# Six column tiles ahead of each norm of the first block, the first transfers in another order, smaller GpSimd pieces, operands shifted by 32 bytes

## The chip, the cores and the metric

The kernel runs on one core of a Trainium2 chip. The core has five engines with queues of their own that run side by side and wait for each other by semaphores: TensorE (PE) multiplies and writes to PSUM, VectorE (DVE) and ScalarE (ACT) work element by element, GpSimd (POOL) helps with element-wise work in SBUF, and SyncE (SP) issues transfers. The metric is the time of one execution on the device in microseconds; of several, the median counts.

## The reference

One sequence of 256 positions with a width of 1024, in float32, goes through two blocks of two layers each. The change is in the first block. Cut to what matters, one of its layers computes

```
h = rms_norm(x, norm1_g)
proj = h @ w_in                     # 1024 x 10312: a (2048), index queries, keys, q, k, v, c, gates
a = causal_dwconv(a_val * sigmoid(a_gate), conf_conv_w) + conf_conv_b        # 31 taps
y_conf = silu(layer_norm(a)) @ w_conf_out
y_attn = dsa_attention(q, k, v, iq, ik, iw) @ w_attn_out                     # top 64 of the causal keys
y_sc = (c_b * causal_dwconv(c_c * c_x, sc_conv_w)) @ w_sc_out
x = x + (gated sum of y_conf, y_attn, y_sc) @ w_o
u = causal_dwconv(rms_norm(x, norm2_g) @ w_up, ffn_conv_w) + ffn_conv_b      # 3 taps
x = x + (silu(u_gate) * u_val) @ w_down                                      # 2816 inner columns
```

with `rms_norm(x, g) = x * rsqrt(mean(x * x) + 1e-6) * g` over the 1024 features of a position. The second block works on these 256 positions and 256 of a context; its very last feed-forward on the 256 positions alone.

## The kernel before

Activations lie transposed: 128 features on the partitions, 8 feature tiles (`KD`), and the positions (`S` = 256) along the free axis. A projection is done one column tile of 128 outputs at a time. `weights` (line 71) fetches one such tile of 128 x 1024 floats (512 KB) over SyncE's queue into one of four `wraw` buffers and splits it into two parts in the faster 32-bit format (float32r): ScalarE copies the rounded value to `whi`, and VectorE or GpSimd subtracts it from the original into `wlo`; each has three buffers. The operand is split in the same way, `oph` and `opl` (later `hh` and `hl`, and in the feed-forwards `dh` and `dl`). `mm` (line 95) then makes 24 matmuls for one column tile: for each of the 8 feature tiles `whi` with `oph` and `whi` with `opl`, and behind them 8 with `wlo` and `oph`. Of the three products that make up float32 accuracy the smallest, low by low, is left out. In the first block a matmul has 256 columns, in the second mostly 512.

`psum` (line 56) sets how many PSUM banks the column tiles and the attention use in a stage, and what share of the weight splits goes to GpSimd: every second one in the first half of a layer (`ps1a`), none in the second (`ps1b`, whose GpSimd splits the feed-forward's `dl` instead). `bank` (line 116) hands out the banks in rotation. Dependencies are tracked by bank in PSUM and by region in SBUF. Work off the main line (the 31 taps, rotary positions, index scores, top-k, softmax) stands in lists of small pieces with an estimated cost; each call of `weights` runs pieces up to a budget of 1600 ns (`run_side`). A scheduler then orders each engine's queue by readiness and priority; `high_priority` moves instructions ahead.

`opening` (line 230) begins each half layer. As the norm's factor `rb` depends on the position alone, a column tile can be multiplied before `rb` is known: `early` (line 204) splits x times the gain, without `rb`, and the tile is multiplied by `rb` in PSUM afterwards. The opening multiplies the first tile so, calls `rms` (line 186: two matmuls with a constant matrix add up the squares over the partitions, ScalarE takes an approximate inverse root, VectorE refines it), then forms the true operand `hn`, split into `hh` and `hl` for all later tiles, and multiplies the other tiles of the opening. It has four tiles in four banks ahead of w_in and three in five banks ahead of w_up. Each tile's multiply by `rb` is VectorE's.

At the start, the four transfers of x (two feature tiles each) alternate between SyncE's and ScalarE's queue, then come the vectors of layer 0 (`vec1[0]`, 490 columns with norm gains, taps and biases), `ident`, `const1` (864 KB of tables) and the weights. `early` and the squares of the norm (`sq_add`, line 159) alternate feature tile by feature tile. The context `z` and the vectors of the second block are loaded at the beginning of layer 1's second half in program order.

Of the kernel before, what the change touches and what calls it, by code (L numbers as in the profile page):

```python
# [21 lines left out]
P = 128  # L22
# [18 lines left out]
class Kern:  # L41
    def __init__(self, tc):
        self.tc = tc
        self.nc = tc.nc
        self.nsplit = 0
        self.pool_share = (0, 1)
        self.jobs = []
        self.job_rate = self.job_due = 0.0
        self.side_hi, self.side_lo = [], []
        self.budget = self.due = 0.0  # L50
        self.mmset, self.atset, self.ps = [], [], None
        self.imm = self.iat = 0
        self.acc, self.last = {}, {}
# [12 lines left out]
    def split(self, hi, lo, src, lo_eng=None):  # L66
        nc = self.nc
        nc.scalar.activation(hi, src, AF.Copy)  # L68
        (lo_eng or nc.vector).tensor_tensor(lo, src, hi.bitcast(F32), op=OP.subtract)  # L69

    def weights(self, src, kt=KD):

        nc = self.nc
# [6 lines left out]
        eng = nc.gpsimd if self.nsplit % of < share else nc.vector  # L80
# [14 lines left out]
    def mm(self, ps, w, xh, xl, kt=KD, k0=0, start=True, stop=True):  # L95

        nc = self.nc
        hi, lo = w
        for k in range(kt):
            nc.tensor.matmul(ps, hi[:, k], xh[:, k0 + k], start=start and k == 0, stop=False)  # L100
            nc.tensor.matmul(ps, hi[:, k], xl[:, k0 + k], start=False, stop=False)  # L101
        for k in range(kt):
            nc.tensor.matmul(ps, lo[:, k], xh[:, k0 + k], start=False, stop=stop and k == kt - 1)  # L103
# [100 lines left out]
def early(K, pool, x, vec, n, k):  # L204

    if k == 0:
        K.early = (pool.tile([P, KD, S], F32R, name="oph", tag="op2h"),
                   pool.tile([P, KD, S], F32R, name="opl", tag="op2l"))
# [6 lines left out]
def first_layer(K, l, A, xz, big, vec1, vec2, cpool, ctx2):  # L215
# [6 lines left out]
    with ExitStack() as ctx:  # L222
        def operand(pool=big, tag="op0"):
            return (pool.tile([P, KD, S], F32R, name="oph", tag=tag + "h"),
                    pool.tile([P, KD, S], F32R, name="opl", tag=tag + "l"))
# [4 lines left out]
        def opening(gname, srcs):  # L230


            banks = []
            for i, src in enumerate(srcs):
                ps = K.bank()[:, :S]
                K.mm(ps, K.weights(src), *K.early)
                if i == 0:
                    rb = K.rms()
                    hh, hl = operand()
                    for k in range(KD):  # L240
                        h = K.np.tile([P, S], F32, name="hn", bufs=3)
                        nc.vector.scalar_tensor_tensor(h, x[:, k], V(gname, k), rb, op0=OP.mult, op1=OP.mult)
                        K.split(hh[:, k], hl[:, k], h)
                nc.vector.tensor_tensor(ps, ps, rb, op=OP.mult)
                banks.append(ps)
            return banks, hh, hl

        with ExitStack() as actx:
            actx.enter_context(K.psum(f"ps1a_{l}", 4, 2, (1, 2)))
            K.budget = 1600.0  # L250
            first, hh, hl = opening("n1", [A["w_in"][l, W_A + i] for i in range(4)])
            if l == 0:
                constants1(K, cpool, A)
                for i in range(1, DEPTH):
                    nc.scalar.dma_start(vec1[i], A["vec1"][i])
# [324 lines left out]
        with ExitStack() as fctx:  # L580
            fctx.enter_context(K.psum(f"ps1b_{l}", 5, 1, (0, 1)))
            first, hh, hl = opening("n2", [A["w_up"][l, i] for i in range(3)])
            ff = fctx.enter_context(tc.tile_pool(name=f"ff1_{l}", bufs=1, reuse_waits="tile"))
            pad(ff, PAD_OP1)
            dh = ff.tile([P, NF, S], F32R, name="dh")
            dl = ff.tile([P, NF, S], F32R, name="dl")
            if l == DEPTH - 1:
# [4 lines left out]
                nc.scalar.dma_start(xz[:, :, S:], A["z"])  # L592
                for i in range(DEPTH):
                    nc.scalar.dma_start(vec2[i], A["vec2"][i])
            for j in range(NF):
# [19 lines left out]
                K.split(dh[:, j], dl[:, j], us[0], nc.gpsimd)  # L615
                if j == 2:
# [20 lines left out]
def constants(K, pool, A):  # L637
    nc = K.nc

    def load(name, shape):  # L640
        t = pool.tile(shape, F32, name=name)
        nc.scalar.dma_start(t, A[name])
        return t
    K.ident = load("ident", [P, P])
# [211 lines left out]
def feed_forward(K, A, x, l, f, T, first, jobs, vec, after, out=None):  # L856

    tc, nc = K.tc, K.nc
    with ExitStack() as ctx:
# [3 lines left out]
        dh = ff.tile([P, NF, T], F32R, name="dh")  # L863
        dl = ff.tile([P, NF, T], F32R, name="dl")
# [49 lines left out]
def pad(pool, size):  # L914

    if size:
        pool.tile([P, size // 4], F32, name="pad")

# [581 lines left out]
def two_blocks_kernel(ctx, tc, A, out):  # L1500
# [66 lines left out]
```

## Time and profile before

| | |
|---|---|
| median of 3 runs | 2945.33 us (2944.72 to 2951.25) |
| profiled execution | 2947.42 us |
| its span, first to last instruction | 2945.6 us |
| mean granted TensorE clock | 0.992 |
| TensorE matmul busy | 2853.4 us (97%), 18738 instructions |
| VectorE busy | 2126.6 us (72%), 3788 instructions |
| ScalarE busy | 1325.6 us (45%), 2189 instructions |
| GpSimd busy | 388.0 us (13%), 225 instructions |
| DMA | 447.64 MB, mean 152 GB/s |

The busy time of an engine is the union of its instructions. Matmuls are pipelined: their ends are modelled and one overlaps the next, so the pace is read from starts. The granted clock is TensorE's share of 2.4 GHz: 0.5 means 1.2 GHz. In the chain that ended last, TensorE has 73%, VectorE 15%, DMA 5% and ScalarE 4% of the span. In a timeline row the bracket says how long the engine was idle before and what ended that.

### The profile page before, as it was taken

Reading aid. Unit: us, or ns where it says so; the run is one execution under the profiler, and the core shown is the slowest. Engines: PE = TensorE matmul, PEld = TensorE weight load, DVE = VectorE, ACT = ScalarE, POOL = GpSimd, SP = SyncE. Lnnn points to the kernel's source line nnn. Section 1 sums busy time; section 2 is a strip of 40 time slices with the busy share of each in tenths; the row PEclk is TensorE's granted clock in tenths of the full one; section 3 lists DMA queues with packets and bytes.
Section 4 is the critical chain, followed back from the end, with each engine's and each line's share of the span. In section 5 each row is a group of like instructions: output and inputs, shape, how many; then the busy total and the mean of one; then the engine's idle time right before and its main releaser. Section 6 shows DMA issues by size and latency. Waiting matters only on the chain.

```text
span 2945.6 us, 47619 instructions
## 1 busy us (share of the span) xinstructions
PE 2853.4 (97%) x18738; PEld 2557.2 (87%) x18738; DVE 2126.6 (72%) x3788; ACT 1325.6 (45%) x2189; POOL 388.0 (13%) x225
## 2 busy tenths in 40 slices
PE   7989999999899999999999899999999999999999
PEld 7889999998899999888788579888888888877999
DVE  7999789789986897777657855777645554484664
ACT  4455666544546655422225454322233322365543
POOL 3333422033234210000000300000000000010000
PEclk9999999999999999999999999999999999999999
DMA  6445556654455576555542112455534444322455
GB/s 206 144 130 162 178 183 222 215 167 138 130 160 180 180 220 215 176 183 171 166 149 95 44 52 73 158 172 169 166 109 161 161 154 142 99 80 74 160 183 152
DMA packets 127935, 447.64 MB, mean 152 GB/s; under 512 B 14304, under 2 KB 19936, under 8 KB 127072
## 3 DMA queue, kind: packets, MB, share of 16 engines
q1 hardware_dynamic: 124672, 439.14, 47.1%
q10 hardware_dynamic: 3040, 5.48, 0.5%
q8 instruction: 147, 2.41, 0.3%
q14 instruction: 76, 0.62, 0.1%
HBM read 443.51 MB, written 1.05 MB: 151 GB/s over the span
## 4 chain that ended last, share of the span: by engine, by line
PE 73%; DVE 15%; DMA 5%; issue 4%; ACT 4%; POOL 0%; SPq 0%; DVEq 0%; ACTq 0%; POOLq 0%
PE mmb L100 21%; PE mmb L101 21%; PE mmb L103 21%; DVE wlo L69 4%; DMA mraw<-in_w_mod_dram 3%; DVE mjunk L770 2%; DMA wraw<-in_w_up_dram 2%; ACT whi L68 1%; PE outb L972 1%; PE atb L939 1%; DVE opl L69 1%; PE mmb L110 1%; PE mmb L111 1%; PE mmb L109 1%; DVE uu L610 1%
## 5 line engine op out<-in xcount | busy, mean ns | idle before, releaser
L68 ACT ACTIVATE whi<-wraw 128x1024 fp32r<-128x1024 f32 (+1 forms) x688 | 714.7, 1041 | 821.6 <-PE mmb L101 624.9
L69 DVE TENSOR_TENSOR wlo<-wraw,whi 128x1024 fp32r<-128x1024 f32 (+1 forms) x575 | 699.7, 1219 | 296.3 <-ACT whi L68 192.1
L100 PE MATMUL mmb<-oph,whi 128*128 128x256 f32 x2512 | 637.1, 290 | 20.8 <-ACT whi L68 12.5
L101 PE MATMUL mmb<-opl,whi 128*128 128x256 f32 x2512 | 630.4, 288 | 5.2 <-DVE opl L69 3.0
L100 PE MATMUL mmb<-hh,whi 128*128 128x512 f32 (+1 forms) x1776 | 613.2, 357 | 1.1 <-ACT whi L68 1.1
L101 PE MATMUL mmb<-hl,whi 128*128 128x512 f32 (+1 forms) x1776 | 610.3, 356 | 0.0
L100 PEld LDWEIGHTS mmb<-oph,whi 128*128 128x128 f32 x2512 | 487.6, 194 | 35.2 <-ACT whi L68 14.7
L101 PEld LDWEIGHTS mmb<-opl,whi 128*128 128x128 f32 x2512 | 488.0, 194 | 13.3 <-DVE opl L69 4.9
L770 DVE SCALAR_TENSOR_TENSOR mjunk<-mraw,cvec 128x1024 f32<-128x1024 f32 x256 | 315.2, 1231 | 223.5 <-DMA mraw<-in_w_mod_dram 217.6
L100 PEld LDWEIGHTS mmb<-hh,whi 128*128 128x128 f32 x1776 | 337.0, 190 | 54.5 <-issue 7.4
L103 PE MATMUL mmb<-hh,wlo 128*128 128x512 f32 (+1 forms) x1776 | 379.1, 355 | 3.2 <-DVE wlo L69 3.2
L101 PEld LDWEIGHTS mmb<-hl,whi 128*128 128x128 f32 x1776 | 336.9, 190 | 48.3 <-issue 2.9
L103 PE MATMUL mmb<-oph,wlo 128*128 128x256 f32 x2512 | 357.8, 285 | 4.0 <-DVE wlo L69 4.0
L69 POOL TENSOR_TENSOR wlo<-wraw,whi 128x1024 fp32r<-128x1024 f32 x113 | 286.1, 2533 | 487.7 <-ACT whi L68 415.9
L100 PE MATMUL mmb<-dh,whi 128*128 128x256 f32 (+1 forms) x1122 | 344.6, 329 | 3.3 <-ACT dh L68 3.3
L101 PE MATMUL mmb<-dl,whi 128*128 128x256 f32 (+1 forms) x1122 | 343.7, 328 | 1.3 <-POOL dl L69 1.3
L103 PEld LDWEIGHTS mmb<-hh,wlo 128*128 128x128 f32 x1776 | 297.9, 189 | 52.5 <-DVE wlo L69 5.3
L103 PEld LDWEIGHTS mmb<-oph,wlo 128*128 128x128 f32 x2512 | 326.7, 193 | 5.8 <-DVE wlo L69 5.2
L100 PEld LDWEIGHTS mmb<-dh,whi 128*128 128x128 f32 x1122 | 214.7, 191 | 22.3 <-ACT dh L68 3.7
L101 PEld LDWEIGHTS mmb<-dl,whi 128*128 128x128 f32 x1122 | 214.6, 191 | 19.9 <-POOL dl L69 1.7
L275 DVE SCALAR_TENSOR_TENSOR cvb<-u,vec,cvb 128x256 f32<-128x256 f32 x480 | 212.6, 481 | 3.5
L103 PE MATMUL mmb<-dh,wlo 128*128 128x256 f32 (+1 forms) x1122 | 210.5, 329 | 1.3 <-DVE wlo L69 1.2
(336 smaller groups left out, 2876.4 us busy)
## 6 DMA issues: line engine op xcount, KB each, us to landing
wraw<-in_w_ff_dram SPq DMA_DIRECT2D x208, 512.0 KB, 3.6
wraw<-in_w_in_dram SPq DMA_DIRECT2D x200, 512.0 KB, 3.6
mraw<-in_w_mod_dram SPq DMA_DIRECT2D x144, 512.0 KB, 4.2
wraw<-in_w_up_dram SPq DMA_DIRECT2D x88, 512.0 KB, 4.3
wraw<-in_w_y_dram SPq DMA_DIRECT2D x64, 512.0 KB, 3.5
wraw<-in_w_ff_dram SPq DMA_DIRECT2D x64, 448.0 KB, 3.4
wraw<-in_w_down_dram SPq DMA_DIRECT2D x32, 448.0 KB, 4.0
wraw<-in_w_down_dram SPq DMA_DIRECT2D x16, 512.0 KB, 4.3
```

The lines of the kernel that those rows point to most:

```text
L68: nc.scalar.activation(hi, src, AF.Copy)
L69: (lo_eng or nc.vector).tensor_tensor(lo, src, hi.bitcast(F32), op=OP.subtract)
L100: nc.tensor.matmul(ps, hi[:, k], xh[:, k0 + k], start=start and k == 0, stop=False)
L101: nc.tensor.matmul(ps, hi[:, k], xl[:, k0 + k], start=False, stop=False)
L103: nc.tensor.matmul(ps, lo[:, k], xh[:, k0 + k], start=False, stop=stop and k == kt - 1)
L109: nc.tensor.matmul(ps, hi[:, k], a, start=start, stop=False)
L110: nc.tensor.matmul(ps, hi[:, k], b, start=False, stop=False)
L111: nc.tensor.matmul(ps, lo[:, k], a, start=False, stop=stop)
L275: nc.vector.scalar_tensor_tensor(box[0], u[:, j, t:t + S], V("cw", 31 * j + t), box[0], op0=OP.mult, op1=OP.add)
L610: nc.vector.scalar_tensor_tensor(uu[:, d:], pe[:, :S - d], V("fw", 3 * t + 2 - d), uu[:, d:], op0=OP.mult, op1=OP.add)
L770: nc.vector.scalar_tensor_tensor(junk, raw, 1.0, K.cvec[:, e], op0=OP.mult, op1=OP.mult, accum_out=K.mods[l][:, e, 8 * m + k:8 * m + k + 1])
L939: nc.tensor.matmul(ps[:, :n], self.q[:, self.pair, tb * P:(tb + 1) * P], self.kpad[:, self.key(e), self.keys[0]:self.keys[1]], start=True, ...
```

## The change

- `opening` takes six column tiles for each norm, in four banks ahead of w_in and five ahead of w_up: tile i lies in bank i mod n, the later ones in the second half of a bank. Tiles 0 and 1 are multiplied for the first seven feature tiles each, then both for the eighth; behind them comes `rms`, the multiply of these two by `rb`, the true operand, and tiles 2 to 5.
- At the start the first eight columns of the vectors (the norm's gains) are fetched first, the first weight tile behind two of the four x transfers and in two halves with a split each, the other vectors behind x. `ident`, `const1` and layer 1's vectors are issued behind the last split of the operand. A Copy of one column right after the constants makes ScalarE load its table. The squares come behind all eight `early` steps.
- A weight split that GpSimd takes is subtracted in four pieces of two feature tiles.
- z and the second block's vectors are issued behind the first Silu of layer 1's feed-forward.
- The operands of 256 columns (first block, and `dh`, `dl` of the last feed-forward) start 32 bytes later, with 32 bytes more behind them.

```diff
+    def load(self, src, kt=KD, cut=KD):
         raw = self.wp.tile([P, KD, P], F32, name="wraw", bufs=4)
-        nc.sync.dma_start(raw[:, :kt], src)
+        cuts = [slice(k, min(k + cut, kt)) for k in range(0, kt, cut)]
+        for c in cuts:
+            nc.sync.dma_start(raw[:, c], src[:, c])
...
-            self.split(hi[:, :kt], lo[:, :kt], raw[:, :kt], eng)
+            if self.nsplit % of < share:
+                for c in cuts:
+                    nc.scalar.activation(hi[:, c], raw[:, c], AF.Copy)
+                for k in range(0, kt, 2):
+                    c = slice(k, min(k + 2, kt))
+                    nc.gpsimd.tensor_tensor(lo[:, c], raw[:, c], hi[:, c].bitcast(F32), op=OP.subtract)
+            else:
+                for c in cuts:
+                    self.split(hi[:, c], lo[:, c], raw[:, c])
...
-        def opening(gname, srcs):
-            banks = []
-            for i, src in enumerate(srcs):
-                ps = K.bank()[:, :S]
-                K.mm(ps, K.weights(src), *K.early)
-                if i == 0:
-                    rb = K.rms()
-                    hh, hl = operand()
-                    for k in range(KD):
...
+        def opening(gname, srcs, n):
+            banks = [K.bank() for _ in range(n)]
+            tiles = [banks[i % n][:, i // n * S:(i // n + 1) * S] for i in range(len(srcs))]
+            two = []
+            for i in range(2):
+                two.append(K.weights(srcs[i]))
+                K.mm(tiles[i], two[i], *K.early, ks=range(KD - 1))
+            for i in range(2):
+                K.mm(tiles[i], two[i], *K.early, ks=(KD - 1,))
+            rb = K.rms()
+            for ps in tiles[:2]:
                 nc.vector.tensor_tensor(ps, ps, rb, op=OP.mult)
+            hh, hl = operand()
+            for k in range(KD):
...
+                act = K.split(hh[:, k], hl[:, k], h)
+            for i, ps in enumerate(tiles[2:], 2):
+                K.mm(ps, K.weights(srcs[i]), *K.early)
+                nc.vector.tensor_tensor(ps, ps, rb, op=OP.mult)
+            K.imm = (K.imm + len(srcs) - n) % len(K.mmset)
+            return tiles, hh, hl, act
...
-            first, hh, hl = opening("n1", [A["w_in"][l, W_A + i] for i in range(4)])
+            first, hh, hl, act = opening("n1", [A["w_in"][l, W_A + i] for i in range(6)], 4)
             if l == 0:
-                constants1(K, cpool, A)
+                with tc.issue_after(act.ins):
+                    nc.scalar.dma_start(K.ident, A["ident"])
+                    constants1(K, cpool, A)
...
-            first, hh, hl = opening("n2", [A["w_up"][l, i] for i in range(3)])
+            first, hh, hl, _ = opening("n2", [A["w_up"][l, i] for i in range(6)], 5)
...
+                if j == 0 and l == DEPTH - 1:
+                    with tc.issue_after(act.ins):
+                        nc.scalar.dma_start(xz[:, :, S:], A["z"])
...
+    nc.scalar.activation(K.np.tile([P, 1], F32, name="nwarm", bufs=2), K.inv[:, 0:1], AF.Copy)
...
+def shifted(pool, shape, **kw):
+    n, w = shape
+    t = pool.tile([P, n * w + 16], F32R, **kw)
+    return t[:, 8:8 + n * w].rearrange("p (a b) -> p a b", b=w)
...
     with tc.high_priority(1000):
+        o, w = V1["n1"]
+        nc.sync.dma_start(vec1[0][:, :o + w], A["vec1"][0][:, :o + w])
         for k in range(0, KD, 2):
             (nc.scalar if k % 4 else nc.sync).dma_start(xz[:, k:k + 2, :S], A["x"][:, k:k + 2])
-        nc.sync.dma_start(vec1[0], A["vec1"][0])
+            if k == 2:
+                K.ahead.append(K.load(A["w_in"][0, W_A], cut=4))
+        nc.scalar.dma_start(vec1[0][:, o + w:], A["vec1"][0][:, o + w:])
     constants(K, keep, A)
     for k in range(KD):
         early(K, big, xz[:, :, :S], vec1[0], "n1", k)
+    for k in range(KD):
         K.sq_add(xz[:, k, :S], k)
```

## Rows read from the trace of the kernel before

**Rows 1.** The page, busy us, share of the span and instructions of each engine.

```profile
PE 2853.4 (97%) x18738; PEld 2557.2 (87%) x18738; DVE 2126.6 (72%) x3788; ACT 1325.6 (45%) x2189; POOL 388.0 (13%) x225
```

**Rows 2.** TensorE's groups by shape: count | busy us, mean ns | idle before.

```profile
L103 PE MATMUL mmb<-oph,wlo 128*128 128x256 f32 x2512 | 357.8, 285 | 4.0 <-DVE wlo L69 4.0
...
L103 PE MATMUL mmb<-dh,wlo 128*128 128x256 f32 x660 | 95.3, 286 | 0.0
```

**Rows 3.** Timeline of TensorE: start us, us, instruction, times in a row.

```profile
19.61 1.91 PE L103 MATMUL mmb<-oph,wlo 128*128 128x256 f32 x8
...
30.16 1.12 PE L103 MATMUL mmb<-oph,wlo 128*128 128x256 f32 x8
...
1203.05 1.98 PE L103 MATMUL mmb<-hh,wlo 128*128 128x512 f32 x8
1204.87 0.39 PE L100 MATMUL mmb<-hh,whi 128*128 128x512 f32 x1
```

**Rows 4.** Timeline of the start; last row: transfers, KB and us to landing.

```profile
1.75 0.46 SPq L1515 DMA_DIRECT2D vec<-in_vec_dram  x1
...
7.37 1.28 ACT L211 ACT_TABLE_LOAD   x1 [7.37 <-DMA vec<-in_vec_dram]
...
10.54 1.06 ACT L68 ACTIVATE whi<-wraw 128x1024 fp32r<-128x1024 f32 x1 [1.37 <-DMA wraw<-in_w_in_dram]
...
11.65 0.58 PE L100 MATMUL mmb<-oph,whi 128*128 128x256 f32 x1 [11.65 <-ACT whi L68]
...
vec<-in_vec_dram SPq DMA_DIRECT2D x1, 245.0 KB, 5.6
```

**Rows 5.** Timeline of TensorE where the norms' operands come late.

```profile
32.23 0.39 PE L100 MATMUL mmb<-oph,whi 128*128 128x256 f32 x1 [0.95 <-ACT th L291]
...
35.19 0.38 PE L100 MATMUL mmb<-oph,whi 128*128 128x256 f32 x1 [1.27 <-ACT oph L68]
...
38.03 0.41 PE L101 MATMUL mmb<-opl,whi 128*128 128x256 f32 x1
...
401.16 0.36 PE L100 MATMUL mmb<-oph,whi 128*128 128x256 f32 x1 [0.61 <-DVE xz L575]
...
603.21 0.39 PE L101 MATMUL mmb<-opl,whi 128*128 128x256 f32 x1 [1.62 <-DVE opl L212]
...
616.06 0.39 PE L100 MATMUL mmb<-oph,whi 128*128 128x256 f32 x1 [2.02 <-ACT th L291]
...
617.13 0.42 PE L101 MATMUL mmb<-opl,whi 128*128 128x256 f32 x1
...
985.56 0.36 PE L100 MATMUL mmb<-oph,whi 128*128 128x256 f32 x1 [0.87 <-DVE xz L575]
```

**Rows 6.** Windows: stretch, its us, then PE, PEld, DVE, ACT, POOL, PEclk, DMA.

```profile
37.00:205.00 168.00, 155.32 (x1179) 145.74 (x1180) 161.08 (x332) 70.89 (x114) 62.95 (x29) 0.97 0.48 148
618.00:785.00 167.00, 154.48 (x1179) 145.37 (x1179) 158.35 (x329) 71.53 (x111) 62.05 (x29) 0.97 0.48 149
```

**Rows 7.** VectorE 37 to 205: ns min/median/max, first and last start; then groups.

```profile
L317 DVE TENSOR_TENSOR iq<-iqr,const x2: 2719/2805/2891, 80.2 to 86.1; 128x512 f32<-128x512 f32 x2
L316 DVE TENSOR_TENSOR ish<-ish,const x2: 678/679/680, 93.4 to 98.3; 128x512 f32<-128x512 f32 x2
...
L69 DVE TENSOR_TENSOR wlo<-wraw,whi x56: 1196/1218/3417, 36.7 to 398.1; 128x1024 fp32r<-128x1024 f32 x56
...
L69 DVE TENSOR_TENSOR wlo<-wraw,whi 128x1024 fp32r<-128x1024 f32 x24 | 34.4, 1432 | 2.2 <-ACT whi L68 2.2
L418 DVE SCALAR_TENSOR_TENSOR ia<-rl,iw,ia 128x256 f32<-128x256 f32 x7 | 7.1, 1014 | 0.0
...
L418 DVE SCALAR_TENSOR_TENSOR ia<-rl,iw,const 128x256 f32<-128x256 f32 x1 | 0.5, 472 | 0.0
```

**Rows 8.** GpSimd's splits of weights (37 to 245) and of the feed-forward's operand.

```profile
L69 POOL TENSOR_TENSOR wlo<-wraw,whi x28: 2343/2407/3697, 41.5 to 241.7; 128x1024 fp32r<-128x1024 f32 x28
...
L69 POOL TENSOR_TENSOR dl<-uu,dh x44: 727/1205/1769, 420.3 to 1127.4; 128x256 fp32r<-128x256 f32 x44
```

More of the change, by code (lines that the diff above doesn't have):

```diff
@@ L52, in __init__ @@
         self.imm = self.iat = 0
-        self.acc, self.last = {}, {}
+        self.acc, self.last, self.ahead = {}, {}, []
     @contextmanager
@@ L67, in split @@
         nc = self.nc
-        nc.scalar.activation(hi, src, AF.Copy)
+        act = nc.scalar.activation(hi, src, AF.Copy)
         (lo_eng or nc.vector).tensor_tensor(lo, src, hi.bitcast(F32), op=OP.subtract)
+        return act
     def weights(self, src, kt=KD):
+        return self.ahead.pop() if self.ahead else self.load(src, kt)
+    def load(self, src, kt=KD, cut=KD):
         nc = self.nc
         raw = self.wp.tile([P, KD, P], F32, name="wraw", bufs=4)
-        nc.sync.dma_start(raw[:, :kt], src)
+        cuts = [slice(k, min(k + cut, kt)) for k in range(0, kt, cut)]
+        for c in cuts:
+            nc.sync.dma_start(raw[:, c], src[:, c])
         hi = self.wp.tile([P, KD, P], F32R, name="whi", bufs=3)
@@ L93, in run_side, with mm @@
         self.due = min(self.due, 0.0) if not (self.side_hi or self.side_lo) else self.due
-    def mm(self, ps, w, xh, xl, kt=KD, k0=0, start=True, stop=True):
+    def mm(self, ps, w, xh, xl, kt=KD, k0=0, start=True, stop=True, ks=None):
         nc = self.nc
         hi, lo = w
-        for k in range(kt):
+        ks = range(kt) if ks is None else ks
+        for k in ks:
             nc.tensor.matmul(ps, hi[:, k], xh[:, k0 + k], start=start and k == 0, stop=False)
             nc.tensor.matmul(ps, hi[:, k], xl[:, k0 + k], start=False, stop=False)
-        for k in range(kt):
+        for k in ks:
             nc.tensor.matmul(ps, lo[:, k], xh[:, k0 + k], start=False, stop=stop and k == kt - 1)
@@ L206, in early @@
     if k == 0:
-        K.early = (pool.tile([P, KD, S], F32R, name="oph", tag="op2h"),
-                   pool.tile([P, KD, S], F32R, name="opl", tag="op2l"))
+        K.early = (shifted(pool, [KD, S], name="oph", tag="op2h"),
+                   shifted(pool, [KD, S], name="opl", tag="op2l"))
     hh, hl = K.early
@@ L250, in first_layer @@
             K.budget = 1600.0
-            first, hh, hl = opening("n1", [A["w_in"][l, W_A + i] for i in range(4)])
+            first, hh, hl, act = opening("n1", [A["w_in"][l, W_A + i] for i in range(6)], 4)
             if l == 0:
-                constants1(K, cpool, A)
-                for i in range(1, DEPTH):
-                    nc.scalar.dma_start(vec1[i], A["vec1"][i])
+                with tc.issue_after(act.ins):
+                    nc.scalar.dma_start(K.ident, A["ident"])
+                    constants1(K, cpool, A)
+                    for i in range(1, DEPTH):
+                        nc.scalar.dma_start(vec1[i], A["vec1"][i])
             opp = actx.enter_context(tc.tile_pool(name=f"op1_{l}", bufs=1, reuse_waits="tile"))
@@ L615, in first_layer @@
                 K.split(dh[:, j], dl[:, j], us[0], nc.gpsimd)
+                if j == 0 and l == DEPTH - 1:
+                    with tc.issue_after(act.ins):
+                        nc.scalar.dma_start(xz[:, :, S:], A["z"])
+                        for i in range(DEPTH):
+                            nc.scalar.dma_start(vec2[i], A["vec2"][i])
                 if j == 2:
@@ L638, in constants @@
     nc = K.nc
[L640 to L644, printed above, removed]
+    K.ident = pool.tile([P, P], F32, name="ident")
     K.inv = pool.tile([P, P], F32, name="inv")
     nc.vector.memset(K.inv, 1.0 / 1024.0)
+    nc.scalar.activation(K.np.tile([P, 1], F32, name="nwarm", bufs=2), K.inv[:, 0:1], AF.Copy)
     K.magic = pool.tile([P, 64], I32, name="magic")
@@ L862, in feed_forward @@
         pad(ff, PAD_FF2)
-        dh = ff.tile([P, NF, T], F32R, name="dh")
-        dl = ff.tile([P, NF, T], F32R, name="dl")
+        dh = shifted(ff, [NF, T], name="dh") if T == S else ff.tile([P, NF, T], F32R, name="dh")
+        dl = shifted(ff, [NF, T], name="dl") if T == S else ff.tile([P, NF, T], F32R, name="dl")
         for j in range(NF):
```

19 lines of the change are left out of this document (6 added, 13 removed).

## The prediction

> **What bounds the kernel now.** I read the page's busy table, then TensorE's groups by shape, then its timeline where it stands idle, then the busy table of the two stages between the norm and the attention, and last VectorE and GpSimd there.
>
> TensorE is busy 97% of the span [rows 1], so its pace and its idle places count. The pace is flat: at full clock eight 256-column matmuls in a row last 1.12 us and a lone one 0.285 [rows 2, 3], so one starts every (1.12 − 0.285) / 7 = 0.119 us, 0.120 in round numbers; eight of 512 columns take 1204.87 − 1203.05 = 1.82, so 0.227 each; at half clock, where a lone one lasts 0.41 [rows 5], the 256-column ones start every (1.91 − 0.41) / 7 = 0.214 [rows 3].
>
> The idle places that the change touches are of three kinds. The start: nothing multiplies until 11.65 us, behind `vec` (245 KB, 5.6 us from issue to landing), a table load of 1.28 us that begins only when `vec` is there at 7.37, and the first weight tile, whose split begins at 10.54 [rows 4]. The places where the norm and its operand come late: 0.95 and 1.27 us in layer 0, 1.62 and 2.02 in layer 1, 0.61 and 0.87 ahead of w_up [rows 5]; behind the first two pairs the clock falls to 1.2 GHz (at 38.03 and 617.13 a matmul lasts 0.41 or 0.42). Third, the stages 37 to 205 and 618 to 785: TensorE works 155.3 of 168 us and 154.5 of 167 at a granted 0.97, VectorE 161.1 and 158.4 [rows 6]. There VectorE is the bound; TensorE's idle 12.7 and 12.5 us, and some 0.03 × 168 = 5 us of clock in each, are all there is to win.
>
> VectorE's time there is partly waiting. Operations with two SBUF inputs last far longer than like ones: `iq` 2.81 us against 0.68 for `ish` of the same shape, `ia` 1.01 against 0.47, `wlo` 1.43 in the mean against 1.20 at best [rows 7]. The surplus fits one GpSimd `wlo` of 2.41 us [rows 8]: VectorE stands until GpSimd's instruction ends. In layer 0 that is 2 × 2.13 + 7 × 0.54 + 24 × 0.23 = 14 us, smaller groups not counted.
>
> **The change part by part.** Gains are counted in the profiled execution (2947.42 us, span 2945.6) and taken off the median of before, 2945.33; the 2.1 us between the two are spread over executions, not over places.
>
> *The start.* The norm's eight gains go first on SP, the first weight tile moves ahead of one x transfer, in two halves, and the rest of `vec`, `ident` and `const1` go behind; a one-element Copy makes the table load at once. Neither load nor `vec` then holds ScalarE. The half weight tile takes about the place on SP that `vec` has now (issued at 1.75, landed at 7.35) with as much data and less before it, so some 6.9; its Copy costs half of 1.06, and an operand Copy or two stand before it. First matmul at 8.1, 3.5 earlier (bounds 2 and 5: 9.7, the half tile no earlier than the table load ended before, and 6.7). The x transfer that it passes carries k = 4 and 5, which come third and fourth in their tile's second half: inside the bounds.
>
> *Two tiles begun by k.* Tile 0 took from 11.65 to 21.5 [rows 3, 4]; 24 matmuls at 0.214 would be 5.1. Of the 4.8 between, some are the norm's own sums, the rest waits for each k, as ScalarE alternates operand, square and a second table load. The squares now come behind all eight operands, and k = 7 of both tiles last: I take 2.0 (0 to 4.8). The norm's sum comes about 0.5 us later for it, but more tiles stand ahead of the first use of its operand.
>
> *Six tiles ahead.* In layer 0 the 0.95 and 1.27 go, and the half clock behind them: 15 matmuls × (0.214 − 0.120) = 1.4. I leave 0.8, for the seventh tile needs a bank that ScalarE and VectorE must first have read: 2.8. Layer 1: 1.62 + 2.02 + 1.4 − 0.8 = 4.2. Ahead of w_up: 0.61 + 0.87 − 0.3 = 1.2. The openings: 3.5 + 2.0 + 2.8 + 4.2 + 1.2 = 13.7 (7 to 19). What is late next is VectorE's chain of operands.
>
> *More multiplies.* Two more in place at the first norm, three at the second, about 0.47 of VectorE each (`ia`'s clean row); in the first they come out of VectorE's account, 0.9 a layer, in the second TensorE's tiles hide them.
>
> *GpSimd's pieces.* Four of 256 elements for one of 1024. The nearest row, `dl`, has 0.73 at best and 1.21 in the middle [rows 8]: 2.9 to 4.8 us for 2.4. Every second tile is GpSimd's, so it has 2 × 24 × 0.12 = 5.76: hidden while a piece stays under 1.44, and TensorE waits for `wlo` beyond. VectorE waits 0.73 at most where it waited up to 2.41: it wins 14 × (1 − 0.73 / 2.41) = 9.8 us a layer. In layer 0 its chain starts about 3 earlier (3.5 of the start, less for the squares that come later), so of 3 + 9.8 − 0.9 it needs 8.3 to keep up with a TensorE that comes 8.3 earlier: 3.6 left. Layer 1: 9.8 − 0.9 − 4.2 = 4.7. Sum 8.3, under the 17 that TensorE could win in each. Bounds: 0 and 2 × 12.
>
> *Transfers moved.* `ident` and `const1` wait on ScalarE's queue for the last operand's split; `const1` is first read at 80.2 [rows 7], long after. The issues cost ScalarE some 0.46 each, as `vec`'s on SP, and ScalarE is not the bound there. z and vec2 leave the first opening, where z's 1 MB ran beside the weights, for layer 1's feed-forward, where nothing but the end of that layer needs them. Nothing; if ScalarE's Copies wait behind the four issues, 2 us once.
>
> *The shift by 32 bytes.* It touches 3 × 2512 + 3 × 660 = 9516 matmuls [rows 2]. No row shows these operands 32 bytes further on, so the two paces bound it: 256 columns more cost 0.227 − 0.120 = 0.107, which leaves 0.013 us of each matmul that no column explains. If the shift removes it, −124 us; if it doubles it, +124. I take zero: all these operands run at 0.120, the 512-column ones, in rows of twice the size, pay the same 0.013, and nothing in the profile moves with an address. The Trainium skill ("TensorE: Matmul & The Clock Gate", Step-by-step: what each phase is for) says that weights and moving operand are read over two independent SBUF ports, so that loading the one takes no bandwidth from the other. By that an address can't help; no run here shows it yet.
>
> Total 13.7 + 8.3 = 22.0; 2945.3 − 22.0 = 2923.
>
> **The rivals.** *The shift pays.* For it: 0.013 of each 0.120 us buys no column; against it: both widths pay it alike. Half of it gone is 62 us, 2861; all is 2799.
>
> *VectorE keeps what it gets.* The pieces only move the waits, GpSimd standing behind VectorE more often. For it: VectorE has 7 us free in 168 [rows 6], and a TensorE that comes earlier waits longer. Some 9 of the openings' 13.7 remain: 2936.
>
> *Two tiles to a bank.* The sixth tile shares a bank with an earlier one, whose readers must stay away while TensorE writes there; so the first pair is read only behind the last tile's multiply, and the readers that free the next bank queue behind it. Layer 1's wait for that reader was 2.02 with 1.4 of half clock [rows 5]; against the 0.8 and 0.3 that I left, four openings cost 2 × 2.6 + 2 × 2.0 = 9 us of the gain: 2932. The Trainium skill ("PSUM — Partial Sum Buffer", PSUM bank collisions raise a hardware error) says to guard by bank, not by address; by that rule tiles in one bank exclude each other though their columns differ. No row here has a bank shared over the norm.
>
> *The other side: the shift costs.* The place is every 256-column matmul that it touches; from 22.0 / 9516 = 2.3 ns each it eats all the rest. At 4 ns 2961, with the 0.013 doubled 3047. For it: the trace knows these operands at one place each, and no pace but this. Against it as above.
>
> **How the numbers follow.** Forecast 0.55, own range 2905 to 2938; shift pays 0.18; VectorE keeps 0.12; banks 0.05; shift costs 0.10. A measurement here tells 0.2% (5.9 us) from no change, so faster is below 2939.4: 0.53 + 0.18 + 0.07 + 0.05 = 0.83; same 0.07; slower 0.10. The range 2836 to 2945 leaves out the costly shift (0.10) and the third of the paying one that lies below (0.06).
>
> **What would show it.** The first matmul near 8 us; no idle over 1 us on TensorE from there to 40 us, nor at the places of 603 and 616; GpSimd's pieces at 0.7 to 1.4 us, `iq` near 1.2; some 5 us less idle on TensorE in the stage after each first norm; eight matmuls still in 1.12 us. If the last is off by 0.03, the forecast is wrong whatever else comes true.

## The result and the profile after

The changed kernel takes 2919.56 us in the median of 5 runs (2918.15 to 2924.06), the kernel before 2945.33 in its 5 beside them: ratio 0.9913, 95% interval 0.9902 to 0.9924, so 25.6 us less (22 to 29). The forecast was 2923. The profiled execution took 2924.06, its span is 2921.9. The total came out; its parts did not, as the next sections show.

The busy table of the page, as [rows 1]:

```profile
PE 2834.6 (97%) x18738; PEld 2542.8 (87%) x18738; DVE 2087.9 (71%) x3799; ACT 1331.9 (46%) x2193; POOL 470.6 (16%) x564
```

TensorE's busy time fell by 18.8 of the 23.7 us of span, at the same mean granted clock, 0.992; so more of the gain lies in matmuls that follow each other faster than in fewer idle places. VectorE works 39 us less with 11 instructions more, GpSimd 83 us more for the same elements.

The timeline of the start, as [rows 4]:

```profile
2.29 1.28 ACT L673 ACT_TABLE_LOAD   x1 [2.29 <-issue]
...
6.93 0.63 ACT L68 ACTIVATE whi<-wraw 128x512 fp32r<-128x512 f32 x1 [3.13 <-DMA wraw<-in_w_in_dram]
...
8.01 0.58 PE L117 MATMUL mmb<-oph,whi 128*128 128x256 f32 x1 [8.01 <-ACT oph L228]
```

The table load no longer waits for `vec`, the half tile is there at 6.93, and the first matmul starts at 8.01 where 8.1 was said. The timeline of TensorE at the four openings, as [rows 5]:

```profile
28.74 1.10 PE L120 MATMUL mmb<-oph,wlo 128*128 128x256 f32 x8
36.07 0.58 PE L117 MATMUL mmb<-oph,whi 128*128 128x256 f32 x1 [6.24 <-ACT th L319]
36.45 0.41 PE L118 MATMUL mmb<-opl,whi 128*128 128x256 f32 x1
...
402.10 1.09 PE L120 MATMUL mmb<-oph,wlo 128*128 128x256 f32 x8
408.19 0.55 PE L117 MATMUL mmb<-oph,whi 128*128 128x256 f32 x1 [5.00 <-DVE uu L635]
408.54 0.41 PE L118 MATMUL mmb<-opl,whi 128*128 128x256 f32 x1
...
603.01 0.62 PE L120 MATMUL mmb<-oph,wlo 128*128 128x256 f32 x3 [2.12 <-DVE wlo L69]
...
607.25 0.58 PE L117 MATMUL mmb<-oph,whi 128*128 128x256 f32 x1 [3.03 <-ACT th L319]
...
978.24 0.55 PE L117 MATMUL mmb<-oph,whi 128*128 128x256 f32 x1 [5.11 <-DVE uu L635]
```

This is the opposite of what was forecast. Before, an opening cost 0.6 to 3.6 us of waits; now each has 5.0 to 6.2, at the tile behind the sixth (at 603.01, 2.12 of them in the sixth, for its lower weights), and the matmuls behind the wait last 0.41, the length that they have at 1.2 GHz. The x8 rows show a second thing: eight matmuls in 1.09 or 1.10 where [rows 3] have 1.12.

Then the two stages between norm and attention as windows with the columns of [rows 6]:

```profile
36.00:192.00 156.00, 149.45 (x1147) 140.52 (x1148) 144.88 (x322) 70.45 (x113) 81.65 (x97) 0.97 0.51 162
...
607.00:764.00 157.00, 149.99 (x1153) 140.99 (x1154) 145.19 (x317) 69.96 (x112) 74.71 (x95) 0.97 0.49 155
```

and VectorE's `iq` and GpSimd's pieces there, by tile, as in [rows 7, 8] (ns min/median/max, first and last start):

```profile
L345 DVE TENSOR_TENSOR iq<-iqr,const x2: 684/684/684, 74.9 to 80.2; 128x512 f32<-128x512 f32 x2
```

```profile
L94 POOL TENSOR_TENSOR wlo<-wraw,whi x116: 718/743/2677, 42.2 to 242.4; 128x256 fp32r<-128x256 f32 x116
```

TensorE's idle in the first falls from 12.7 to 6.5 us, in the second from 12.5 to 7.0. A piece lasts 0.743. `iq` lasts 0.684 in place of 2.81, but GpSimd stands idle beside it in this execution, so this row says nothing of pieces; a row that does comes further down.

Three questions follow: do the pieces carry all of it; what do six tiles cost, and why; does the shift pay.

### The profile page after: what moved, and what is told of

Same layout as the page of the kernel before. It is cut to its first block, busy times and chain, and to the rows that moved or that the text cites. A ratio compares the mean times of both kernels' runs of the same rounds, so it can differ in the third digit from the quotient of the medians.

```text
span 2921.9 us, 48073 instructions
## 1 busy us (share of the span) xinstructions
PE 2834.6 (97%) x18738; PEld 2542.8 (87%) x18738; DVE 2087.9 (71%) x3799; ACT 1331.9 (46%) x2193; POOL 470.6 (16%) x564
## 3 DMA queue, kind: packets, MB, share of 16 engines
q8 instruction: 147, 2.41, 0.3%
## 4 chain that ended last, share of the span: by engine, by line
PE 60%; DVE 9%; DMA 3%; issue 3%; ACT 2%; POOL 0%; DVEq 0%; ACTq 0%; SPq 0%
PE mmb L117 17%; PE mmb L120 17%; PE mmb L118 17%; DMA mraw<-in_w_mod_dram 2%; DVE wlo L69 2%; DVE mjunk L797 2%; PE outb L1006 1%; PE atb L973 1%; PE mmb L127 1%; PE mmb L128 1%; PE mmb L126 1%; DMA wraw<-in_w_up_dram 1%; ACT whi L68 1%; DVE ks L1175 1%; PE mmb L1001 1%
## 5 line engine op out<-in xcount | busy, mean ns | idle before, releaser
L68 ACT ACTIVATE whi<-wraw 128x1024 fp32r<-128x1024 f32 (+2 forms) x576 | 596.5, 1038 | 725.5 <-PE mmb L118 570.3
L69 DVE TENSOR_TENSOR wlo<-wraw,whi 128x1024 fp32r<-128x1024 f32 (+2 forms) x576 | 698.8, 1215 | 313.0 <-ACT whi L68 208.6
L117 PEld LDWEIGHTS mmb<-oph,whi 128*128 128x128 f32 x2512 | 480.3, 191 | 43.6 <-issue 20.5
L118 PEld LDWEIGHTS mmb<-opl,whi 128*128 128x128 f32 x2512 | 481.8, 192 | 5.3 <-issue 3.7
L94 POOL TENSOR_TENSOR wlo<-wraw,whi 128x256 fp32r<-128x256 f32 x452 | 370.2, 851 | 396.8 <-ACT whi L90 375.6
```

The costliest lines, as they stand in the source:

```text
L68: act = nc.scalar.activation(hi, src, AF.Copy)
L94: nc.gpsimd.tensor_tensor(lo[:, c], raw[:, c], hi[:, c].bitcast(F32), op=OP.subtract)
```

## Experiments: each part by itself

The four parts, each alone on the kernel before; ratios are to that kernel beside them (2943.54 in 27 runs).

```
shift_only    early(), operand(), dh, dl:  pool.tile(...)  ->  shifted(pool, ...)
pieces_only   + for k in range(0, kt, 2): gpsimd.tensor_tensor(lo[:, k:k+2], raw[:, k:k+2], hi[:, k:k+2], subtract)
start_only    + order of the first transfers, K.ahead, nwarm, squares behind early(), issue_after; opening of before
six_only      + opening(..., 6 tiles, 4 banks) and (..., 6 tiles, 5 banks), two tiles begun by k
```

> The kernel before with the operands of 256 columns lying 32 bytes further on, and nothing else. Theory A (the forecast): no matmul's pace depends on it, 2945, within 5 us of before. Theory B (the shift pays a little on each matmul, and the six tiles lose): the 256-column matmuls that are touched start every 0.118 us in the middle in place of 0.120, so 9516 x 0.0015 to 0.002 = 14 to 19 us less, 2926 to 2931.

> The kernel before with GpSimd's lower weight halves in four pieces, and nothing else. Theory A: VectorE's waits shrink and TensorE, whose start is where it was, wins 4 to 9 us over the two layers: 2936 to 2941. Theory B says 2 to 6 us, since the stalls on v's and the probabilities' operand (vn, pr) of before, some 14 us together, stay in large part. A rival (VectorE keeps what it gets): within 2 us of before.

> The kernel before with the new order of the first transfers, the first weight tile ahead and in halves, the early table load, the squares behind the operand, ident, const1, z and vec2 deferred, and the opening of before (four and three tiles, each from k = 0 to 7). Theory A: 3.5 us at the start and part of the 2.0 of the operand, kept to the end: 2940 to 2942. Theory B: some 6 us by the third operand tile as in the changed kernel's trace, of which VectorE's chain in the first stage takes a part: 2939 to 2943. A rival: all is eaten by that chain, within 2 us of before.

> The kernel before with the new opening (first two tiles begun by k, six tiles ahead in four or five banks, two banks shared) and nothing else. Theory A: 10 us faster with the start's 2 of the operand (2.0 + 2.8 + 4.2 + 1.2), 2935. Theory B: the readers of the first pair wait until the last tile that shares their bank is multiplied, so each of the four openings has one wait of 5 to 6 us and 7 us of half clock where before had waits of 0.6 to 3.6: 3 to 7 us lost at each, of which VectorE's and the banks' slack give some back: slower by 5 to 20 us, 2950 to 2965.

Measured:

```
              median us   ratio, 95% interval        us to before
shift_only    2940.69     0.9994  0.9985 to 1.0003    -1.8
pieces_only   2922.03     0.9924  0.9910 to 0.9937   -22.4
start_only    2943.37     1.0003  0.9994 to 1.0012    +0.9
six_only      2952.53     1.0028  1.0020 to 1.0037    +8.2
all (change)  2919.56     0.9913  0.9902 to 0.9924   -25.6
```

The pieces alone make nearly the whole gain, far above what either theory gave them. The start alone is worth nothing (its rival), six tiles alone cost 8 (theory B), the shift alone is within its interval of nothing (theory A; theory B's 14 to 19 are out). The four sum to -15.1, the change has -25.6: some 10 us appear only in company. The five intervals, each about 3 us either way, make that uncertain by some 7.

**Where the pieces gain.** Windows of the kernel before and, below each, of the kernel with the pieces alone, cut so that both hold the same matmuls: the first stage of layer 0, the stage behind it, and the first stage of layer 1.

```profile
37.18:221.14 183.96, 171.28 (x1284) 160.37 (x1284) 175.52 (x365) 85.56 (x158) 65.45 (x31) 0.96 0.47 145
36.74:208.85 172.11, 167.29 (x1284) 157.10 (x1284) 162.52 (x365) 86.25 (x158) 84.27 (x106) 0.99 0.48 156
...
221.14:375.21 154.07, 153.95 (x1252) 151.05 (x1251) 133.26 (x219) 85.87 (x137) 60.94 (x26) 1.00 0.56 171
208.85:363.04 154.19, 153.91 (x1252) 151.06 (x1251) 121.06 (x220) 86.13 (x138) 79.18 (x101) 1.00 0.53 170
...
618.19:830.37 212.18, 198.13 (x1463) 184.06 (x1463) 201.04 (x415) 102.05 (x187) 72.77 (x35) 0.96 0.45 141
605.49:805.42 199.93, 192.85 (x1463) 179.40 (x1463) 187.53 (x413) 102.23 (x187) 90.84 (x119) 0.99 0.46 147
```

The first stage is 11.9 us shorter: VectorE needs 13.0 us less for the same 365 instructions, TensorE's idle falls from 12.7 to 4.8, its granted clock rises from 0.96 to 0.99. In the stage behind it VectorE needs 12.2 us less and nothing is won, for TensorE was hardly ever idle there. Layer 1's first stage is 12.3 us shorter. The two make 24.1 of the 24.4 us between the two spans. Summed over both layers, VectorE's instructions that run more than 0.15 us over the shortest tenth of their kind have 52.8 us of surplus with the pieces against 102.8 before (from 11 to 380 and 600 to 965; by line, operation and shape).

**Why the start alone gives nothing.** VectorE's timeline behind the first norm, in start_only and, below it, in a kernel with the same start and the pieces (four_three, further down; it has the shift too); last, ScalarE's in start_only:

```profile
19.50 0.41 DVE L208 SCALAR_TENSOR_TENSOR nrr<-atb,nry 128x256 f32<-128x256 f32 x1
19.95 2.18 DVE L209 TENSOR_TENSOR nrr<-nrr,nry 128x256 f32<-128x256 f32 x1
...
24.82 3.36 DVE L257 SCALAR_TENSOR_TENSOR hn<-xz,vec,nry 128x256 f32<-128x256 f32 x3
...
34.17 0.74 DVE L309 SCALAR_TENSOR_TENSOR u<-th,mmb 128x256 f32<-128x256 f32 x2
```

```profile
21.45 0.52 DVE L211 TENSOR_TENSOR nrr<-nrr,nry 128x256 f32<-128x256 f32 x1
...
26.75 0.40 DVE L320 SCALAR_TENSOR_TENSOR u<-th,mmb 128x256 f32<-128x256 f32 x1
```

```profile
30.35 0.35 ACTq L269 DMA_DIRECT2D ident<-in_ident_dram  x1
30.73 0.45 ACTq L670 DMA_DIRECT2D const<-in_const_dram  x1
31.21 0.45 ACTq L272 DMA_DIRECT2D vec<-in_vec_dram  x1
31.70 1.28 ACT L308 ACT_TABLE_LOAD   x1 [0.94 <-issue]
32.99 0.38 ACT L308 ACTIVATE th<-mmb 128x256 f32<-128x256 f32 x1
```

and in the kernel before:

```profile
23.28 2.12 DVE L194 TENSOR_TENSOR nrr<-nrr,nry 128x256 f32<-128x256 f32 x1
...
31.80 0.38 ACT L291 ACTIVATE th<-mmb 128x256 f32<-128x256 f32 x1
```

The norm's first step on VectorE (`nrr`) comes at 19.50 where before it came at 22.82, but ScalarE's first `th` at 32.99 for 31.80, and TensorE, which needs the bank that `th` reads, waits 7.72 us until 33.43; before it waited 0.95 and 1.27. The lead is lost on two engines. VectorE's steps stand behind whole GpSimd instructions: the step of 2.18 does so before too (2.12), the three `hn` of 3.36 come on top (before, the six `hn` ahead of the first `th` take 1.28 and 1.27 by threes). And ScalarE issues the three moved transfers, 1.3 us, and loads a table ahead of `th`. No run tells the two apart. TensorE's 48th matmul starts 5.6 us earlier than before (19.19 for 24.76), the 150th 0.3 (41.97 for 42.24). In four_three, where `u` comes at 26.75 and the issues behind the first `th`, the 150th starts at 34.71, 5.9 us ahead of the kernel with the pieces alone (40.58). So in company the start's lead is kept that far (with two tiles begun by k, which four_three has too), and alone the rival "VectorE keeps what it gets" fits it, with ScalarE's part added.

## Experiments: the length of a piece, and who shares a bank

```
pieces_of_512, pieces_of_128   pieces_only with range(0, kt, 4) and range(0, kt, 1)
own_banks    the change with  opening("n1", 4 tiles, 4)  and  opening("n2", 5 tiles, 5)
pair_banks   the change with tiles (0) (1) (2,3) (4,5) to the four banks, (0) (1) (2) (3) (4,5) to the five; next bank is the first
```

> The kernel before with GpSimd's lower halves in two pieces of 512 elements, and nothing else. Theory A (what pays is that VectorE waits only until GpSimd's running instruction ends): a piece lasts some 1.25 us by 2.41 for 1024 and 0.74 for 256, so VectorE waits half as long, and the gain is some two thirds of that of pieces of 256 (22): 12 to 17 us, 2927 to 2932. Theory B (the gain comes from the first half of the weights being there earlier, or from the new order of the instructions): as with 256, 2919 to 2924, or nothing, 2943.

> The kernel before with GpSimd's lower halves in eight pieces of 128 elements, and nothing else. Theory A: a piece lasts some 0.45 us (0.74 less the 0.56 / 2 that 128 elements cost by 2.41 less 0.74 for 768), so VectorE waits less still, GpSimd's tile takes 3.6 us of its 5.8: 2 to 6 us under pieces of 256, 2916 to 2920. Rival: GpSimd becomes the bound, as each piece waits its turn behind VectorE's instructions (0.4 each): 8 x 0.85 = 6.8 us a tile over 5.8, TensorE waits for the lower halves, and it is 2925 to 2945.

> The changed kernel with four tiles ahead of the first norm and five ahead of the second, so that no bank is shared; the rest of the change stays. Theory A (sharing costs: the readers of the first pair stand behind the last tile's multiply, and the tile after the sixth waits for them): the waits of 5 to 6 us at the four openings shrink to 1 to 2, of which some was caught up later in the changed kernel; 5 to 15 us under it, 2905 to 2915. Theory B (the chain of operands on VectorE sets when the stage can go on, however many tiles stand ahead): within 4 us of the changed kernel, 2916 to 2924.

> The changed kernel with six tiles ahead as it has them, but the two tiles that share a bank are tiles that are read together (2 with 3, 4 with 5; at the second norm 4 with 5), and the tile after the sixth takes the first bank. Theory A: the readers of the first pair no longer wait by the bank; what is left is VectorE's order (the first pair's reader stands behind the sixth multiply), so a wait of 1.5 to 3 us in place of 5 to 6 at each opening, 2908 to 2917. Theory B (VectorE's order and chain set it, not the bank): the waits stay at 5 to 6 us, 2917 to 2923.

Measured, beside 2944.32 for the kernel before (11 runs):

```
               median us   ratio, 95% interval        us to before
pieces_of_512  2930.51     0.9948  0.9933 to 0.9963   -15.3
pieces_of_128  2919.86     0.9913  0.9898 to 0.9929   -25.6
own_banks      2917.51     0.9902  0.9887 to 0.9917   -28.9
pair_banks     2921.44     0.9918  0.9904 to 0.9932   -24.1
```

**The dose.** GpSimd's group from 35 to 365 (busy, mean ns of one) in the kernel before and in those with pieces of 512, 256 and 128 elements:

```profile
L69 POOL TENSOR_TENSOR wlo<-wraw,whi 128x1024 fp32r<-128x1024 f32 x49 | 123.2, 2514 | 177.3 <-ACT whi L68 144.1 <-DVE cvb L275 16.7 <-DVE mx L455 6.9
```

```profile
L88 POOL TENSOR_TENSOR wlo<-wraw,whi 128x512 fp32r<-128x512 f32 x99 | 138.5, 1420 | 173.5 <-ACT whi L85 151.1 <-DVE cvb L281 7.8 <-ACT whi L68 6.8
```

```profile
L88 POOL TENSOR_TENSOR wlo<-wraw,whi 128x256 fp32r<-128x256 f32 x204 | 166.2, 845 | 151.2 <-ACT whi L85 146.6 <-ACT whi L68 4.3
```

```profile
L88 POOL TENSOR_TENSOR wlo<-wraw,whi 128x128 fp32r<-128x128 f32 x407 | 219.7, 577 | 110.7 <-ACT whi L85 105.7 <-ACT whi L68 4.6 <-POOL yv L506 0.4
```

A mean instruction of GpSimd of 2.51, 1.42, 0.85 and 0.58 us leaves VectorE a surplus of 102.8, 80.2, 52.8 and 37.9 us (counted as above) and makes the kernel 0, 15.3, 22.4 and 25.6 faster. Both kernels lie where theory A put them, and the order is one that only it has; the last step, from 256 to 128, is within the intervals. What pays is the length of the instruction that VectorE stands behind. One operation shows it, `iq`, before and with the pieces of 256:

```profile
79.94 2.40 POOL L69 TENSOR_TENSOR wlo<-wraw,whi 128x1024 fp32r<-128x1024 f32 x1 [3.30 <-DVE cvb L275]
80.17 2.72 DVE L317 TENSOR_TENSOR iq<-iqr,const 128x512 f32<-128x512 f32 x1
```

```profile
78.28 0.74 POOL L88 TENSOR_TENSOR wlo<-wraw,whi 128x256 fp32r<-128x256 f32 x1 [2.88 <-ACT whi L85]
78.59 0.98 DVE L323 TENSOR_TENSOR iq<-iqr,const 128x512 f32<-128x512 f32 x1
```

Both times `iq` begins while GpSimd works and ends 0.55 us after that instruction of GpSimd has ended (82.89 for 82.34, 79.57 for 79.02); with GpSimd idle it lasts 0.684. The Trainium skill ("Trainium Architecture — The Big Picture", What this means for kernel authors) says that VectorE and GpSimd share a pair of ports as an exclusive lock, not a split of bandwidth; the trace agrees (`iq` 2.72 behind a whole instruction, 0.98 behind a piece). GpSimd pays for it with idle time that it had: its busy time goes from 388.0 to 581.9 with eight pieces, and the kernel is no slower for it.

**The bank.** Theory A wanted 2905 to 2915 of own_banks and 2908 to 2917 of pair_banks; both medians lie with theory B, though own_banks' interval (2911 to 2920) takes in both, so the waits have to decide. TensorE's timeline at the two openings of w_up in own_banks, where five tiles have a bank each, behind its longest wait at w_in of layer 0, where four have:

```profile
27.29 0.39 PE L117 MATMUL mmb<-oph,whi 128*128 128x256 f32 x1 [1.90 <-DVE u L320]
...
398.79 0.55 PE L117 MATMUL mmb<-oph,whi 128*128 128x256 f32 x1 [6.00 <-DVE uu L635]
...
969.34 0.55 PE L117 MATMUL mmb<-oph,whi 128*128 128x256 f32 x1 [5.61 <-DVE uu L635]
```

and in pair_banks at w_up of layer 0 and w_in of layer 1:

```profile
396.33 0.55 PE L117 MATMUL mmb<-oph,whi 128*128 128x256 f32 x1 [3.37 <-DVE mmb L270]
...
602.03 0.58 PE L117 MATMUL mmb<-oph,whi 128*128 128x256 f32 x1 [7.05 <-DVE mmb L270]
```

No bank is shared in the first, and at w_up its wait for the reader `uu` is as long as with six: all five banks are taken, and the reader that frees the first stands on VectorE behind the operands and the multiplies of all the tiles ahead. So there a shared bank isn't why the tile behind the sixth waits, and theory A falls. At w_in own_banks' waits did shrink, to 0.47 and 1.90 for 6.24 in layer 0 and to 1.32, 0.94 and 1.76 for 2.12 and 3.03 in layer 1; but it has two tiles fewer there as well, and no run tells the two apart. In pair_banks the waits move: TensorE, before it writes the second half of a bank, waits for the multiply of the first half (L270), 2.14, 3.37, 7.05 and 3.37 at the four openings. So a shared bank costs where it lies, and the waits did not stay at the 5 to 6 of theory B either.

## Experiments: the tiles of before, and the shift once more

```
four_three            the change with  opening("n1", 4 tiles, 4)  and  opening("n2", 3 tiles, 3)
four_three_128        and GpSimd's pieces of 128
four_three_no_shift   and  return t[:, 0:n * w]  in place of  t[:, 8:8 + n * w]  (tiles as large)
four_three_shift_all  and hh, hl, dh, dl of the second block's 512 columns shifted too
```

> The changed kernel with four tiles ahead of the first norm and three ahead of the second, as the kernel before had; the rest of the change stays. Theory A (a tile that stands ahead takes a bank and puts one more multiply in front of the readers, so the tile behind the last of them waits; with five of five banks taken this was 6.0 and 5.6 us at w_up): those two waits fall to under 1 us; layer 0's was caught up by the end of its w_up, layer 1's was not, so 5 us under five tiles (2917.5), 2910 to 2914. Theory B (tiles ahead cost nothing in the end): 2915 to 2920.

> The kernel four_three with GpSimd's lower halves in eight pieces of 128 elements. Theory A (VectorE's wait is one piece long): 1 to 4 us under four_three, as 128 against 256 alone (24 against 22). Rival: with TensorE earlier, the longer tile of GpSimd (eight pieces) is what TensorE waits for, 0 to 5 us over it.

> The kernel four_three with the operands of 256 columns in the same enlarged tiles, but at their start (no shift). Theory A (the shift takes 0.1 to 1.9 ns off each matmul, 1.3 in the mean over the operands as the traces show, but only stages in which TensorE is the bound keep it): with VectorE no longer the bound, 4 to 12 us over four_three. Theory B (the pace differs between neighbours only, the sum doesn't): within 2 us of it, as the shift alone was.

> The kernel four_three with the second block's operands of 512 columns (hh, hl, dh, dl) 32 bytes further on too. Theory A (a matmul gains the same 1.3 ns whatever its columns): some 4600 of 512 columns and 2400 of 256, in a block where TensorE is the bound throughout: 5 to 10 us under four_three. Theory B (the long ones gain nothing, or the gain isn't kept): only the 256-column ones gain, 0 to 3 us under it.

Measured, beside 2945.42 (9 runs):

```
                      median us   ratio, 95% interval
four_three            2914.39     0.9896  0.9882 to 0.9909
four_three_128        2916.69     0.9902  0.9888 to 0.9915
four_three_no_shift   2914.04     0.9893  0.9879 to 0.9906
four_three_shift_all  2936.12     0.9965  0.9951 to 0.9979
```

**four_three** and its twin without the shift are the fastest kernels here: some 5 us under the changed kernel, though the intervals still overlap. The step from five tiles to three at w_up is 3 us by the medians, 2 by the ratios, between the two theories and not told apart. Its wait at w_up did not fall under 1 us; its timeline has

```profile
390.77 0.79 PE L117 MATMUL mmb<-oph,whi 128*128 128x256 f32 x2 [3.50 <-ACT oph L68]
```

and now the operand is late, not a bank. The reason shows in TensorE's rows at this place of the changed kernel and of pieces_only, which has the opening of before:

```profile
385.01 0.36 PE L117 MATMUL mmb<-oph,whi 128*128 128x256 f32 x1 [0.61 <-DVE xz L603]
...
390.76 0.59 PE L199 MATMUL atb<-nacc,inv 128*128 128x256 f32 x2
```

```profile
387.62 0.35 PE L106 MATMUL mmb<-oph,whi 128*128 128x256 f32 x1 [0.61 <-DVE xz L581]
...
390.56 0.59 PE L188 MATMUL atb<-nacc,inv 128*128 128x256 f32 x2
```

The norm's sum stands behind two tiles (48 matmuls) instead of one: 5.75 us behind the first matmul in place of 2.94. Every operand and multiply of the opening waits for that sum, so the new order starts VectorE's chain 2.8 us later at w_up; the forecast spoke of 0.5, and at the start only.

**The pieces of 128** give nothing more here (theory A's 1 to 4 us are not seen, and the rival's loss, 2.3 us by the medians, is within the intervals).

**The shift** makes no difference between the two: 2914.39 with it, 2914.04 without. But they are no clean pair. The mean distance from one 256-column matmul on these operands to the next (100 to 150 ns counted) is 119.91 ns before, 118.64 in shift_only, 118.59 in four_three and 118.76 in four_three_no_shift, whose tiles begin where they would but are 64 bytes larger. So the pace does move with where the operands lie, and enlarging the tiles alone moves it as much. 1.3 ns by 9516 is 12 us, of which shift_only kept 1.8, at most 4.4. Where TensorE is never idle, the gain is there in time; the same 800 matmuls of layer 0 before, in the changed kernel and in four_three_no_shift:

```profile
248.66:345.21 96.55, 96.55 (x802) 96.39 (x801) 85.19 (x136) 51.32 (x79) 39.94 (x17) 1.00 0.58 176
```

```profile
236.11:331.08 94.97, 94.97 (x802) 94.81 (x801) 79.39 (x148) 51.77 (x80) 51.73 (x67) 1.00 0.56 179
```

```profile
227.99:323.42 95.43, 95.43 (x802) 95.28 (x801) 74.79 (x138) 51.72 (x80) 51.48 (x66) 1.00 0.56 179
```

shift_only needs 94.97 too, pieces_only 96.55. What becomes of it depends on the next wait: from the 1401st matmul of the program to the 2701st shift_only takes 162.9 us for 162.7 before, as TensorE waits 2.13 at 376.34 for an operand (before 1.67 at 378.15), while the changed kernel, which has no such wait, takes 159.0 for 161.4 in pieces_only. So some 2 us of the shift reach the second norm in layer 0 of the changed kernel, and in layer 1 its 1000 matmuls from the 6001st take 118.7 for 120.6 alike. Whether they are kept to the end stays open: a kernel with the pieces, the new start and the old layout was not run.

In **four_three_shift_all** theory A fails in its sign. TensorE's timeline, eight matmuls of 512 columns and the next, against 1.82 us from start to start in [rows 3]:

```profile
1202.39 2.04 PE L120 MATMUL mmb<-hh,wlo 128*128 128x512 f32 x8
1204.27 0.39 PE L117 MATMUL mmb<-hh,whi 128*128 128x512 f32 x1
```

That is 1.88 from start to start, 0.235 each; in the mean over the kernel it is 0.233 for 0.227, and 0.006 x 4938 (three groups of 1184 and three of 462) is 30 us. The kernel is 21.7 slower, and TensorE's busy time 21.5 longer (2861.2 for 2839.7); the 256-column matmuls of that block gain a little against it.

## Why the prediction was right in sum, and wrong in its terms

**The start** (3.5): the first matmul came at 8.01 for 8.1. But alone it is worth +0.9 (-1.8 to 3.5): its lead is gone by the 150th matmul. The step that failed is that a gain at the first matmul is a gain at the end, whatever stands on VectorE and ScalarE behind it. With the pieces it is kept at least that far.

**Six tiles ahead, two of them by k** (2.8 + 4.2 + 1.2, and 2.0 of the start): measured alone +8.2, so the sign is wrong. The two tiles by k did what was said: in six_only the 48th matmul comes 2.6 us earlier than before (22.13 for 24.76). The loss comes behind them. The step that failed is "I leave 0.8, for the seventh tile needs a bank that ScalarE and VectorE must first have read". That reader was priced as if it came when its own pair was ready; it comes on VectorE behind six multiplies, eight operands and the splits of weights, and the sum that starts all these is 2.8 us later at w_up. Measured: 6.24, 5.15 (2.12 + 3.03), 5.00 and 5.11, and half clock behind them. The waits to be saved were misread too. Of the six in [rows 5] only the 1.27 is for an operand behind the norm: 0.95 and 2.02 are already for such a reader (`th`), and 1.62, 0.61 and 0.87 stand ahead of a first tile, for `early`'s operand and for x itself; the wait for x is 0.61 at both w_up after the change (385.01, 954.94). The rival "Two tiles to a bank" named the place and 9 us, but at w_up its mechanism is not the one: without a shared bank the wait is 6.00.

**GpSimd's pieces** (8.3): measured alone 22.4 (18.5 to 26.5). The place and the mechanism were right: the gain lies in the two stages that the prediction named, and the dose shows what makes it. The size was not, by two steps. VectorE won 13.0 us in layer 0's stage and 13.5 in layer 1's, where 9.8 were counted, "smaller groups not counted". And of 2 × 9.8 the forecast kept 8.3, as VectorE "needs 8.3 to keep up with a TensorE that comes 8.3 earlier", and 4.2 in layer 1: this is the step that failed. In four_three TensorE's 200th matmul comes 7.6 us earlier than before (40.65 for 48.24) and the 1401st 19.3 (201.81 for 221.15); the earlier start and the stage's gain add up. The bound of 2 × 12 held the 22.4.

**The shift** (0): shift_only is -1.8 (-4.4 to 0.9), so alone the time agrees. The reasoning was wrong: "by that an address can't help". Two ports, as the Trainium skill's page "TensorE: Matmul & The Clock Gate" (Step-by-step: what each phase is for) has them, do not make the pace blind to the address: 119.9 became 118.6, and 227 became 233. In the changed kernel some 2 us of it reach the second norm in each layer, which a term of 0 leaves out. The test "eight matmuls still in 1.12" came out at 1.09 to 1.12, so at the lowest it is off by the 0.03 that was to make the forecast wrong.

**Transfers moved** (0): not measured apart from the start. None of TensorE's waits in the changed kernel's list is for z or vec2. But "if ScalarE's Copies wait behind the four issues, 2 us once" is near what start_only shows, 1.3 us of issues ahead of `th`. In the changed kernel the issues stand there too (32.73 to 34.04, table load to 35.35), but the multiply of the sixth tile ends at 34.83, so at most 0.5 of the 6.24 is theirs.

So 13.7 + 8.3 = 22.0 was met by 22.4 for the pieces, -8.2 for the tiles, some 0 for start and shift alone, and 10 us that exist only in company: two terms wrong by about 14 and 18 us, in opposite directions. That the sum came out is luck.

## What to carry to other kernels

When an engine's operations last longer than like ones, add up all of that surplus, small groups too, in the stages where this engine is the bound, before pricing its cure; where another engine is never idle the cure pays nothing (12.2 us less of VectorE's time, and none of the kernel's). Here four GpSimd instructions for one, no other work changed, made most of the change's gain. Work put ahead of a late operand covers it only if the chain behind it does not start later and the buffers that it takes come free in time: look where the norm's sum and the first reader stand in each engine's order. And when one engine sets the pace, measure a gain upstream together with the cure for that engine; alone it may read as nothing.

## What the runs showed of the hardware

The pace of a matmul depends on where the moving operand lies: with tiles moved by 32 bytes, or only 64 bytes larger, the mean distance of 256-column ones went from 119.9 to 118.6 or 118.8 ns and spread (5% to 95%: 120 to 120 before, 115 to 122 for `oph,wlo` in shift_only); with 512 columns it went from 227 to 233. No run told what address rule is behind it.

GpSimd's subtraction takes 2.41 us in the median for 1024 elements, 1.30 for 512, 0.74 for 256 and 0.46 for 128 (35 to 365; before, pieces_of_512, pieces_only, pieces_of_128): a piece of an eighth costs a fifth. VectorE's `iq`, begun meanwhile, ended 0.55 us after GpSimd's instruction, whether that was a whole one or a piece.

Executions of one kernel differ by a few us: the kernel before had 2940.1 to 2951.0 in 27 runs, and its profiled execution, 2947.42, lies in the upper part. Parts of 5 us read off two spans are not results; the ratios above are.
